# Three-stage attention: scores per head, raw probabilities turned, a column of ones beside the values

## The chip, the cores and the metric

One core of one Trainium2 chip runs the whole program. The metric is the device time of one execution in microseconds (us).

## What is computed

Two blocks run one after the other on 256 tokens of width 1024, in float32. The first has two layers. Layer 0 mixes the tokens by a sparse attention with three branches (compressed, selected, window; called NSA here), layer 1 by a block attention on shared keys (MoBA); each is followed by a mixture of 32 experts and a gated embedding (PLE). The second block has a feed-forward part, a mixer (half pooling, half dilated attention) and another feed-forward part, all modulated by a vector. At 256 tokens each of the three attentions reads all its causal keys, so the part that the change rewrites is, for every head,

```python
s = q @ k.T - slopes * dist
s = jnp.where(mask, s, -jnp.inf)
e = jnp.exp(s - m)
o = (e / jnp.maximum(jnp.sum(e, axis=axis, keepdims=True), 1e-30)) @ v
```

with 16 heads of 64 in NSA (two such branches and the compressed one, each times its gate, are added) and in MoBA, and 8 heads in the mixer, where the exponentials are also multiplied by a table of weights (several dilations fall on the same key).

## The kernel before

The weights stream in by DMA on SyncE's queue into nine buffers of 2048 columns (tag `raw`). Dense products (L305 to L307) split both factors into a high and a low part and take three passes of matmuls. Instructions are recorded in program order, and a scheduler then sets the order on each engine; K holds its hints. Matmuls that have nothing to do with attention stand among the attention's: compressed scores (L698, L716), the transposes of the normalised queries (L348), pieces of the modulation vector (L1448, L1461, called by `fill`), and products with the output weights as soon as an eighth of the input is there.

Attention works in units of two neighbouring heads (index `j`) and one branch. NSA has 8 pairs with two branches, 16 units; MoBA has 8 units, the mixer 4. Queries lie turned, the dimensions of both heads on 128 partitions. `keys` makes a tile with two copies of the keys, each with zeros in place of the other head's 64 dimensions (L545 on GpSimd, POOL), so that one matmul with 128x128 weights gives the scores of both heads: L566 for the first 128 queries and keys, L568 for the other queries and all 256 keys. Then, unit by unit:

- VectorE (DVE) adds slope times distance and takes the minimum in one instruction per block (L575, four blocks: 128 or 256 keys, two heads). ScalarE (ACT) takes the exponential and the sum of each row (L580); in the mixer DVE multiplies by the table and sums (L583).
- DVE turns the sums into factors w (L586, L587; L589 multiplies NSA's gate into them), and the probabilities are scaled by w in place: one block on ACT (L593), three on DVE (L595).
- The matrix engine (PE) turns them by six transposes (L599 to L601), and ACT copies them out of PSUM (L602, two copies).
- `attend` (L609, L611) multiplies with the values as weights, 64 columns for each head, so that the two heads fill the two halves of the output partitions and the result is already turned. In NSA the second branch and the compressed one (L782, tiles of 32 rows) add into the same PSUM tile. `parts` (L300 on ACT, L301 on DVE) splits it for the product with the output weights.

`pair` (L773) does this for NSA, loops in `moba` (L831) and `mixer` (L1580) for the others. After pair 1 the second half of the queries is normalised, turned and put through the compressed softmax (`q_norm`, `q_T`, `compressed_softmax`), which puts a chain of DVE work between the units. PSUM has two sets of four banks, `psa` (scores) and `psb`.

Of the kernel before, what the change touches and what calls it, by code (L numbers as in the profile page):

```python
# [43 lines left out]
    sw='svvv',  # L44
# [153 lines left out]
class Block:  # L198
# [343 lines left out]
    def keys(self):  # L542
        kb = self.raw.tile([P, 4, 2, T], F32, tag="raw", name="kb")
        for hf in range(2):
            self.nc.gpsimd.memset(kb[64 * hf:64 * hf + 64, :, 1 - hf], 0.0)  # L545
        return kb

    def put_k(self, idx, ps, gain):

        nc = self.nc  # L550
        for hf, eng in ((0, "s"), (1, "v")):
            sl = slice(64 * hf, 64 * hf + 64)
            dst = self.KB[idx // 4][sl, idx % 4:idx % 4 + 2, hf, :]
            if gain is None:
                self.copy(dst, ps[sl])
            elif eng == "s":
                nc.scalar.activation(dst, ps[sl], AF.Identity, scale=gain[sl])
            else:
                nc.vector.tensor_scalar(dst, ps[sl], gain[sl], None, op0=OP.mult)

    def softmax_T(self, j, kb, QT, slopes, dist, mult, gate):

        nc = self.nc
        with self.ahead_by("soft"):
# [5 lines left out]
            p = self.pp_p.tile([P, 6 * P], F32, tag="p", name="p")  # L570
            p0, p1 = p[:, 0:2 * P].rearrange("p (h k) -> p h k", h=2), p[:, 2 * P:].rearrange("p (h k) -> p h k", h=2)
            blocks = [(p0[:, 0], s0[:, 0], P, 2 * P), (p0[:, 1], s0[:, 1], P, 2 * P),
                      (p1[:, 0], s1[:, 0], 0, 2 * P), (p1[:, 1], s1[:, 1], 0, 2 * P)]
            for i, (p, s, a, b) in enumerate(blocks):
                nc.vector.tensor_tensor_reduce(out=p, in0=s, in1=dist[:, a:b], scale=-float(slopes[2 * j + i % 2]),  # L575
                                               scalar=3e38, op0=OP.add, op1=OP.min, accum_out=m[:, i:i + 1])
            den = self.stat([P, 4], "den")
# [142 lines left out]
    def nsa(self):  # L720
# [74 lines left out]
        for j in range(8):  # L795
            pair(j)
            if j == K["norm_a"]:
                self.q_norm(q[1])
# [869 lines left out]
```

## Time and profile before

| | us |
|---|---|
| median of 3 runs (lowest to highest) | 1142.69 (1141.37 to 1143.42) |
| the profiled execution | 1141.74 |
| its span, first to last instruction | 1139.9 |
| PE busy (of the span) | 1061.5 (93%) |
| weight loads (PEld) busy | 830.7 (73%) |
| DVE busy | 729.1 (64%) |
| ACT busy | 514.6 (45%) |
| POOL busy | 74.8 (7%) |
| mean granted clock of PE | 0.973 of full |

Matmuls overlap, and the end of each in the trace is modelled, so differences between starts tell what a stream of them costs. A float32 matmul takes two passes and leaves two records, a transpose one. A wait on PEld is one of a weight load, which comes ahead of its matmul.

### The profile page before, as it was taken

To read this page: it belongs to the slowest core of one execution; us is meant where nothing else is said; L and a number is where in the kernel's file an instruction comes from. 1 tells how busy PE (TensorE), PEld (TensorE's weight loads), DVE (VectorE), ACT (ScalarE), POOL (GpSimd) and SP (SyncE) were. 2 spreads that over 40 slices of the span, in tenths; PEclk is the share of its full clock that TensorE was granted. 3 is DMA by queue.
4 is the path that set the end of the run, shared out by engine and by line. 5 is a ranking of instruction groups with operands and counts; after the bars stand their busy time and mean duration, and the time that the engine had idled before them with its cause. 6 is when DMAs were issued, how large, how long until landed. Compare 5 with 4: busy or idle time off the path is not lost.

```text
span 1139.9 us, 18296 instructions
## 1 busy us (share of the span) xinstructions
PE 1061.5 (93%) x7037; PEld 830.7 (73%) x7037; DVE 729.1 (64%) x1717; ACT 514.6 (45%) x992; POOL 74.8 (7%) x61
## 2 busy tenths in 40 slices
PE   7997999998899899998987999999989979999995
PEld 5884557564467667665555999999879759999994
DVE  6787866542379957343377587878674776554555
ACT  5446774221267774321253443443544634444443
POOL 3000002100010002000003000000210030000001
PEclk9998999997999999999998999999989989999998
DMA  9755464899964635898886468786674344454401
GB/s 372 287 194 223 186 231 154 300 383 371 350 245 166 245 126 187 327 372 318 333 322 265 148 239 332 302 308 252 234 300 168 129 184 145 169 189 164 141 26 38
DMA packets 46507, 268.55 MB, mean 236 GB/s; under 512 B 5328, under 2 KB 7120, under 8 KB 20432
## 3 DMA queue, kind: packets, MB, share of 16 engines
q1 hardware_dynamic: 46416, 267.34, 62.4%
q8 instruction: 57, 0.93, 0.3%
q14 instruction: 34, 0.28, 0.1%
HBM read 266.27 MB, written 1.05 MB: 235 GB/s over the span
## 4 chain that ended last, share of the span: by engine, by line
PE 47%; DVE 5%; ACT 1%; issue 0%; ACTq 0%; DVEq 0%
PE b L306 8%; PE b L305 8%; PE b L307 8%; PE a L305 5%; PE a L307 5%; PE a L306 5%; PE a L1055 1%; DVE nq L320 1%; PE b L1461 1%; DVE h L1484 1%; PE a L1095 1%; PE a L1108 1%; DVE rstd L324 1%; DVE w L1483 1%; PE b L1034 0%
## 5 line engine op out<-in xcount | busy, mean ns | idle before, releaser
L293 DVE TENSOR_TENSOR lo<-raw,hi 128x1024 fp32r<-128x1024 f32 (+2 forms) x220 | 255.9, 1167 | 166.5 <-ACT hi L292 165.7
L292 ACT ACTIVATE hi<-raw 128x1024 fp32r<-128x1024 f32 (+2 forms) x234 | 234.3, 1008 | 266.2 <-PE b L306 142.5
L305 PE MATMUL b<-e,hi 128*128 128x256 f32 x768 | 219.8, 286 | 2.9 <-ACT e L427 2.9
L306 PE MATMUL b<-e,hi 128*128 128x256 f32 x768 | 219.5, 286 | 0.1
L307 PE MATMUL b<-e,lo 128*128 128x256 f32 x768 | 219.1, 285 | 0.0
L305 PE MATMUL a<-hi,e 128*128 128x512 f32 (+2 forms) x512 | 201.5, 394 | 2.4 <-ACT e L365 1.8
L307 PE MATMUL a<-hi,e 128*128 128x512 f32 (+2 forms) x512 | 198.4, 390 | 0.5 <-DVE e L366 0.5
L306 PE MATMUL a<-lo,e 128*128 128x512 f32 (+2 forms) x512 | 198.9, 388 | 0.0
L305 PEld LDWEIGHTS b<-e,hi 128*128 128x128 f32 x768 | 149.4, 195 | 3.9 <-ACT e L427 3.6
L306 PEld LDWEIGHTS b<-e,hi 128*128 128x128 f32 x768 | 149.4, 194 | 1.0 <-DVE e L428 0.7
L307 PEld LDWEIGHTS b<-e,lo 128*128 128x128 f32 x768 | 149.3, 194 | 0.0
L305 PEld LDWEIGHTS a<-hi,e 128*128 128x128 f32 x512 | 97.4, 190 | 23.2 <-ACT e L365 2.9
L307 PEld LDWEIGHTS a<-hi,e 128*128 128x128 f32 x512 | 96.7, 190 | 21.3 <-DVE e L366 2.1
L306 PEld LDWEIGHTS a<-lo,e 128*128 128x128 f32 x512 | 97.6, 191 | 19.0 <-DVE lo L293 0.9
L1055 PE MATMUL a<-raw,e 128*32 128x256 f32 x832 | 78.6, 399 | 5.5 <-PEq L1314 5.4
L1055 PEld LDWEIGHTS a<-raw,e 128*32 128x32 f32 x832 | 32.2, 113 | 23.9 <-issue 9.0
L1439 DVE SCALAR_TENSOR_TENSOR w<-raw,c,w 128x512 f32<-128x512 f32 x63 | 45.7, 747 | 0.6
L485 DVE TENSOR_TENSOR h<-h,a 128x512 f32<-128x512 f32 x48 | 31.9, 684 | 21.0 <-PE a L1108 14.4
L580 ACT ACTIVATE p<-p,m 128x128 f32<-128x128 f32 (+1 forms) x96 | 42.6, 447 | 5.5 <-DVE m L575 4.4
L293 POOL TENSOR_TENSOR lo<-raw,hi 128x1024 fp32r<-128x1024 f32 (+1 forms) x14 | 31.4, 2263 | 206.1 <-ACT hi L292 206.0
L1098 ACT ACTIVATE w<-a,sv 128x512 fp32r<-128x512 f32 x32 | 21.6, 687 | 50.0 <-PE a L1095 49.0
L1084 ACT ACTIVATE hb<-a,rr 128x128 f32<-128x128 f32 x16 | 6.0, 373 | 83.6 <-DVE rr L1024 77.2
(321 smaller groups left out, 1455.9 us busy)
## 6 DMA issues: line engine op xcount, KB each, us to landing
raw<-in_ffn SPq DMA_DIRECT2D x62, 1024.0 KB, 4.8
raw<-in_moe_gu SPq DMA_DIRECT2D x52, 1024.0 KB, 7.3
raw<-in_w_ada SPq DMA_DIRECT2D x36, 1024.0 KB, 6.7
wd<-in_moe_dn SPq DMA_DIRECT2D x64, 512.0 KB, 6.1
raw<-in_w_gate SPq DMA_DIRECT2D x8, 1024.0 KB, 10.8
raw<-in_w_m_in SPq DMA_DIRECT2D x8, 1024.0 KB, 7.3
raw<-in_w_a_in SPq DMA_DIRECT2D x7, 1024.0 KB, 11.0
e<-in_moe_gu SPq DMA_DIRECT2D x6, 1024.0 KB, 6.7
```

The source lines that it names most:

```text
L292: nc.scalar.activation(hi[:, sl], raw[:, at], AF.Copy)
L293: eng.tensor_tensor(lo[:, sl], raw[:, at], hi[:, sl], op=OP.subtract)
L305: mm(out, l[0], r[0], start=start, stop=False, **kw)
L306: mm(out, l[0], r[1], start=False, stop=False, **kw)
L307: mm(out, l[1], r[0], start=False, stop=stop, **kw)
L320: nc.vector.scalar_tensor_tensor(q, y, h, y, op0=OP.mult, op1=OP.mult)
L324: nc.vector.scalar_tensor_tensor(y, q, 1.5, y, op0=OP.add, op1=OP.mult)
L485: self.nc.vector.tensor_tensor(self.h[:, t, sl], self.h[:, t, sl], ps, op=OP.add)
L580: nc.scalar.activation(p, p, AF.Exp, bias=m[:, i:i + 1], scale=-1.0, accum_out=den[:, i:i + 1])
L1055: nc.tensor.matmul(pgs[pp][32 * x:32 * x + 32], xg[:, k, o:o + 32], wg[kk][:, x], start=(k == 0), stop=(k == KT - 1))
L1098: nc.scalar.activation(yh[:, sl], py, AF.Identity, scale=cw)
L1439: eng.scalar_tensor_tensor(rows, w, by, rows, op0=OP.mult, op1=OP.add)
```

## The change

`softmax_T` and `attend` give way to one function, `attention`, which runs a list of units through three stages: the scores of unit i, the transposes of unit i-1, the products of unit i-2, and then whatever stands beside it (`beside`: the fills and the second half of the queries).

- Scores are four matmuls over 64 rows each, for each head and each half of the queries, into one PSUM tile a head; the first half of the queries meets 128 keys only. The keys are stored once, without zeros, so `keys` loses its two POOL fills, and `put_k` writes all 128 partitions in one instruction (in NSA one buffer holds both branches).
- The exponentials keep no sums and are turned unscaled. `values` puts a column of ones behind each head's 64, so that the product (L607 to L609, turned probabilities as weights, 65 columns moving) brings the sum along with the output, queries on partitions. DVE takes the maximum with 1e-30, the reciprocal and the gate (L611, L612, L614) and scales the output out of PSUM (L616).
- In NSA POOL adds the two branches (L618), and the sum is turned by a matmul against the identity (L811) into the PSUM tile into which the compressed branch was multiplied (L808, as L782 before). In MoBA and the mixer two transposes (L639) turn it.
- Small tiles are shared to make room (`le`, `full`).

```diff
-    def softmax_T(self, j, kb, QT, slopes, dist, mult, gate):
...
-            s0 = self.psa([P, 2, P])
-            nc.tensor.matmul(s0, QT[:, j, 0:P], kb[:, :, 0:P], start=True, stop=True)
-            s1 = self.psa([P, 2, T])
-            nc.tensor.matmul(s1, QT[:, j, P:T], kb, start=True, stop=True)
...
+    def keys(self, n):
+        kb = self.raw.tile([P, n, 4, T], F32, tag="raw", name="kb")
+        self.KB = [kb[:, i] for i in range(n)]
...
+    def values(self, groups, tail):
+        n = 2 * groups * 65
+        t = self.e([P, 2064])
+        v = t[:, 0:n].rearrange("p (t g d) -> p t g d", t=2, d=65)
+        self.nc.gpsimd.memset(v[:, :, :, 64:65], 1.0)
+        return v, t[:, n:n + tail]
+
+    def attention(self, units, QT, slopes, dist, mult, finish, beside):
...
+        def scores(u):
+            j, kb, _, _, _ = units[u]
+            s = [self.psa([P, 3 * P]) for _ in range(2)]
+            for t in range(2):
+                for hh in range(2):
+                    sl = slice(64 * hh, 64 * hh + 64)
+                    mm(s[hh][:, t * P:t * P + (t + 1) * P], QT[sl, j, t * P:(t + 1) * P], kb[sl, 0:(t + 1) * P],
+                       start=True, stop=True)
...
+            for i, (o, x, a) in enumerate(blocks):
+                nc.scalar.activation(o, o, AF.Exp, bias=m[:, i:i + 1], scale=-1.0)
+                if mult is not None:
+                    nc.vector.tensor_tensor(o, o, mult[:, a:2 * P], op=OP.mult)
+            live[u] = p
+
+        def turn(u):
...
+                for k in range(3):
+                    nc.tensor.transpose(ps[:, k * P:(k + 1) * P], p[:, hh, k * P:(k + 1) * P], self.ident)
+                nc.scalar.activation(pT[:, hh], ps, AF.Copy)
...
+        def products(u):
+            j, _, v, gate, last = units[u]
+            pT = live.pop(u)
+            ps = self.psb([P, 2, 2, 65])
+            for hh in range(2):
+                mm(ps[:, 0, hh], pT[:, hh, 0:P], v(0, hh), start=hh == 0, stop=True, skip_group_check=True)
+                mm(ps[:, 1, hh], pT[:, hh, P:2 * P], v(0, hh), start=False, stop=False, skip_group_check=True)
+                mm(ps[:, 1, hh], pT[:, hh, 2 * P:], v(1, hh), start=False, stop=True, skip_group_check=True)
+            w = self.stat([P, 2, 2, 1], "w")
+            nc.vector.tensor_scalar(w, ps[:, :, :, 64:65], 1e-30, None, op0=OP.max)
+            nc.vector.reciprocal(w, w)
+            if gate is not None:
+                nc.vector.tensor_tensor(w[:, :, :, 0], w[:, :, :, 0], gate, op=OP.mult)
+            o = self.wk.tile([P, 2, 2, 64], F32, tag="xn", name="o", bufs=4)
+            nc.vector.tensor_tensor(o, ps[:, :, :, 0:64], w.to_broadcast([P, 2, 2, 64]), op=OP.mult)
+            if j in rows:
+                nc.gpsimd.tensor_tensor(o, o, rows.pop(j), op=OP.add)
+            if last:
+                finish(j, o.rearrange("p t h d -> p t (h d)"))
+            else:
+                rows[j] = o
+
+        n = len(units)
+        for i in range(n + 2):
+            if i < n:
+                scores(i)
+            if 1 <= i <= n:
+                turn(i - 1)
+            if i >= 2:
+                products(i - 2)
+            beside(i)
...
             for hh in range(2):
...
+                nc.tensor.matmul(oT[64 * hh:64 * hh + 64], self.VC[c:c + 32, g], PC[c:c + 32, g], start=True, stop=False,
+                                 skip_group_check=True)
+            for t in range(2):
+                nc.tensor.matmul(oT[:, t * P:(t + 1) * P], o[:, t], self.ident, start=False, stop=True,
+                                 skip_group_check=True)
             self.parts(aT[0][:, j], aT[1][:, j], oT)
```

Where the instructions stand. In these listings, names read output<-inputs: `a` and `b` are PSUM tiles, `kb` keys, `e` on a score matmul the queries and on a product the values, `p` and `pT` probabilities before and after turning; `consts` holds the identity and the distances.

The first listing is PE in the opening of NSA, behind the first scores; before:

```order
L568 MATMUL a<-kb,e 128x512
L566 MATMUL a<-kb,e 128x256
L568 MATMUL a<-kb,e 128x512
L1448 MATMUL a<-raw,c_701 32x512 x8
L566 MATMUL a<-kb,e 128x256
L716 MATMUL b<-consts,pc 128x128 x2
L568 MATMUL a<-kb,e 128x512
L716 MATMUL b<-consts,pc 128x128 x2
L566 MATMUL a<-kb,e 128x256
L599 MATMUL b<-consts,p 128x128
L600 MATMUL b<-consts,p 128x128
```

and now:

```order
L577 MATMUL a<-kb,e 128x128
L577 MATMUL a<-kb,e 128x256 x2
L577 MATMUL a<-kb,e 128x128 x2
L577 MATMUL a<-kb,e 128x256 x2
L1484 MATMUL a<-raw,c_693 32x512
L746 MATMUL b<-consts,pc 128x128 x2
L598 MATMUL b<-consts,p 128x128 x3
L746 MATMUL b<-consts,pc 128x128 x2
L598 MATMUL b<-consts,p 128x128 x3
L1484 MATMUL a<-raw,c_693 32x512 x7
L577 MATMUL a<-kb,e 128x128 x2
```

The scores of two units now stand in front, pieces of the modulation and the compressed products (L716, now L746) come later, and the first transposes stand between and behind the two compressed products; the third unit's scores follow them.

The second listing is PE in the steady part of NSA, with the numbers of the tiles; before:

```order
L601 MATMUL b_1264<-consts_88,p_1245 128x128
L599 MATMUL b_1269<-consts_88,p_1245 128x128
L600 MATMUL b_1269<-consts_88,p_1245 128x128
L601 MATMUL b_1269<-consts_88,p_1245 128x128
L1461 MATMUL b_1297<-consts_88,w4_1295 128x1 x4
L609 MATMUL b_1201<-pT_1263,e_240 64x256 x2
L611 MATMUL b_1201<-pT_1263,e_240 64x128 x2
L782 MATMUL b_1201<-e_240,vc_96 64x256 x2
```

and now:

```order
L808 MATMUL b_1464<-e_240,vc_96 64x256 x2
L577 MATMUL a_1471<-kb_457,e_689 128x128
L577 MATMUL a_1472<-kb_457,e_689 128x128
L577 MATMUL a_1471<-kb_457,e_689 128x256
L577 MATMUL a_1472<-kb_457,e_689 128x256
L811 MATMUL b_1464<-consts_88,o_1461 128x128 x2
L598 MATMUL b_1488<-consts_88,p_1430 128x128 x3
L598 MATMUL b_1493<-consts_88,p_1430 128x128 x3
L607 MATMUL b_1498<-e_240,pT_1439 128x65
L608 MATMUL b_1498<-e_240,pT_1439 128x65
L609 MATMUL b_1498<-e_240,pT_1439 128x65
```

Before, only a piece of the modulation (L1461) stands between the transposes of `p_1245` and the products with `pT_1263`, which is the same unit. Now the products behind the transposes of `p_1430` are with `pT_1439`, turned from the unit ahead of it (`p_1390`), and the second output step L811 stands behind one unit's scores.

The third listing is DVE in the same place; before:

```order
L586 TENSOR_SCALAR den_1352<-den_1352 128x4
L575 ISA p_1414,m_1413<-a_1411,consts_88 128x256
L575 ISA m_1413 128x1
L587 RECIPROCAL w_1357<-den_1352 128x4
L589 TENSOR_TENSOR w_1357<-w_1357,gates_242 128x4
L595 TENSOR_SCALAR p_1347<-p_1347,w_1357 128x128
L595 TENSOR_SCALAR p_1347<-p_1347,w_1357 128x256 x2
L586 TENSOR_SCALAR den_1419<-den_1419 128x4
L587 RECIPROCAL w_1424<-den_1419 128x4
L589 TENSOR_TENSOR w_1424<-w_1424,gates_242 128x4
L595 TENSOR_SCALAR p_1414<-p_1414,w_1424 128x128
L595 TENSOR_SCALAR p_1414<-p_1414,w_1424 128x256
```

and now:

```order
L584 ISA p_1430,m_1429<-a_1423,consts_88 128x256
L584 ISA m_1429 128x1
L584 ISA p_1430,m_1429<-a_1424,consts_88 128x128
L584 ISA m_1429 128x1
L584 ISA p_1430,m_1429<-a_1424,consts_88 128x256
L584 ISA m_1429 128x1
L611 TENSOR_SCALAR w_1457<-b_1450 128x4
L612 RECIPROCAL w_1457<-w_1457 128x4
L614 TENSOR_TENSOR w_1457<-w_1457,gates_243 128x4
L616 TENSOR_TENSOR o_1461<-b_1450,w_1457 128x256
L584 ISA p_1478,m_1477<-a_1471,consts_88 128x128
L584 ISA m_1477 128x1
```

L595 is gone. The small operations L611 to L614 and the scaled copy L616 now stand behind the minima of the unit whose scores PE made before these products, and ahead of the next unit's.

## Rows read from the trace of the kernel before

**Rows 1.** The page's first part: busy us, share of the span, instructions.

```profile
PE 1061.5 (93%) x7037; PEld 830.7 (73%) x7037; DVE 729.1 (64%) x1717; ACT 514.6 (45%) x992; POOL 74.8 (7%) x61
```

**Rows 2.** Busy by stretch: us, PE, PEld, DVE, ACT, POOL, PEclk, DMA share, GB/s.

```profile
84.90:170.50 85.60, 78.64 (x478) 45.20 (x478) 62.48 (x302) 61.48 (x202) 0.00 (x0) 0.96 0.56 213
384.00:423.00 39.00, 32.70 (x173) 21.00 (x173) 28.81 (x135) 31.00 (x104) 0.00 (x0) 1.00 0.55 205
883.60:907.60 24.00, 23.71 (x127) 17.16 (x126) 20.87 (x97) 16.95 (x40) 0.00 (x0) 1.00 0.28 106
```

**Rows 3.** Waits of the DMA queue, 150 to 320 us: us, times, longest us.

```profile
SPq L275 <- PE a L1055: 35.9, 13, 6.3
```

**Rows 4.** Waits of the weight loads in NSA: us, times, longest us.

```profile
PEld b L599 <- ACT p L593: 7.5, 5, 5.1
PEld b L609 <- ACT pT L602: 5.7, 12, 0.8
```

**Rows 5.** Waits of the weight loads in MoBA.

```profile
PEld b L609 <- ACT pT L602: 4.9, 14, 0.7
PEld b L599 <- ACT p L593: 4.5, 4, 2.3
```

**Rows 6.** Waits of the weight loads in the mixer.

```profile
PEld b L609 <- ACT pT L602: 2.0, 6, 0.5
```

**Rows 7.** Timeline, PE in the mixer: start us, us, instruction.

```profile
888.85 0.60 PE L566 MATMUL a<-kb,e 128*128 128x256 f32 x2
889.28 1.02 PE L568 MATMUL a<-kb,e 128*128 128x512 f32 x2
890.14 0.59 PE L1576 MATMUL b<-pool,w 128*128 128x256 f32 x2
...
892.95 0.27 PE L599 MATMUL b<-consts,p 128*128 128x128 f32 x1
...
893.49 0.27 PE L601 MATMUL b<-consts,p 128*128 128x128 f32 x1
894.06 0.81 PE L609 MATMUL b<-pT,e 128*64 128x256 f32 x3 [0.29 <-ACT pT L602]
```

**Rows 8.** Timeline, PE in NSA's opening: idle before in brackets.

```profile
104.75 0.69 PE L599 MATMUL b<-consts,p 128*128 128x128 f32 x2 [4.62 <-ACT p L593]
```

**Rows 9.** Busy by stretch around that wait, columns as rows 2.

```profile
99.70:104.80 5.10, 0.48 (x5) 0.05 (x1) 5.00 (x29) 5.00 (x16) 0.00 (x0) 0.73 0.39 165
104.80:108.50 3.70, 3.39 (x14) 1.98 (x14) 2.93 (x8) 1.27 (x3) 0.00 (x0) 0.50 0.27 35
```

**Rows 10.** Timeline, PE in NSA's steady part.

```profile
129.87 0.95 PE L1461 MATMUL b<-consts,w 128*128 128x1 f32 x8
130.75 0.65 PE L609 MATMUL b<-pT,e 128*64 128x256 f32 x4
131.24 0.39 PE L611 MATMUL b<-pT,e 128*64 128x128 f32 x4
131.55 0.65 PE L782 MATMUL b<-e,vc 32*64 32x256 f32 x4
```

**Rows 11.** Groups by shape in NSA: busy us, mean ns, idle before, releaser.

```profile
L580 ACT ACTIVATION_READ_ACCUMULATOR p<-p,m 128x1 f32 x64 | 12.2, 191 | 0.0
...
L595 DVE TENSOR_SCALAR p<-p,w 128x256 f32<-128x256 f32 x32 | 9.9, 347 | 0.0
...
L593 ACT ACTIVATE p<-p,w 128x128 f32<-128x128 f32 x16 | 6.3, 396 | 1.8 <-DVE w L589 1.8
...
L595 DVE TENSOR_SCALAR p<-p,w 128x128 f32<-128x128 f32 x16 | 4.5, 282 | 0.3
...
L587 DVE RECIPROCAL w<-den 128x4 f32<-128x4 f32 x16 | 2.8, 174 | 0.2
...
L701 DVE TENSOR_TENSOR pc<-a,consts 128x256 f32<-128x256 f32 x4 | 1.6, 420 | 0.3 <-PE a L698 0.2
```

**Rows 12.** Groups by shape on POOL, whole span.

```profile
L1005 POOL TENSOR_TENSOR G<-G,G 128x256 fp32r<-128x256 f32 x16 | 11.7, 731 | 158.9 <-DVE G L1003 141.4 <-DVE slg L1189 9.1 <-DVE rr L1025 6.1
```

More of the change, by code (lines that the diff above doesn't have):

```diff
@@ L605, in attend @@
-    def attend(self, oT, pT, v, start, stop):
-        mm = self.nc.tensor.matmul
-        for hh in range(2):
-            mm(oT[64 * hh:64 * hh + 64, :], v(0, hh), pT[:, hh, 0:T], start=start, stop=False)
-        for hh in range(2):
-            mm(oT[64 * hh:64 * hh + 64, P:T], v(1, hh), pT[:, hh, T:], start=False, stop=stop)
+            live[u] = pT
+        def products(u):
[17 more added lines that the diff above has]
+                finish(j, o.rearrange("p t h d -> p t (h d)"))
+            else:
+                rows[j] = o
@@ new lines, in attention, with out_T, put @@
+        n = len(units)
[7 more added lines that the diff above has]
+            beside(i)
+    def out_T(self, aT, j0):
+        def put(j, o):
+            oT = self.psb([P, T])
+            for t in range(2):
+                self.nc.tensor.transpose(oT[:, t * P:(t + 1) * P], o[:, t], self.ident)
+            self.parts(aT[0][:, j0 + j], aT[1][:, j0 + j], oT)
+        return put
@@ L763, in nsa @@
         next(compress)
-        self.KB = [self.keys() for _ in range(2)]
+        self.keys(2)
         self.k_T(0, ks, self.s("a_k_norm1"))
@@ L794, in nsa @@
         aT = (self.e([P, KT, T], F32R), self.e([P, KT, T], F32R))
[L795 to L798, printed above, removed]
-            if j == K["early_a"]:
-                self.q_T(QT, 1, q[1], qg)
-                self.compressed_softmax(1, QT, gates, PC)
-            self.fill("nsa", j)
-            if j == K["proj"]:
-                self.project_load(0)
+        units = [(j, self.KB[br][:, j // 2], lambda t, hh, br=br, g=j // 2: V[:, br, t, g],
+                  gates[:, :, 2 * j:2 * j + 2, 1 + br], br == 1) for j in range(8) for br in range(2)]
+        self.attention(units, QT, self.slopes, self.c("dist"), None, out, beside)
         self.moe(0, aT, "w_a_out")
@@ L830, in moba, with beside @@
         aT = (self.e([P, KT, T], F32R), self.e([P, KT, T], F32R))
-        for j in range(8):
-            g = j // 2
-            oT = self.psb([P, T])
-            pT = self.softmax_T(j, self.KB[0][:, g], QT, self.slopes, self.c("dist"), None, None)
-            self.attend(oT, pT, lambda t, hh: V[:, t, 64 * g:64 * g + 64], True, True)
-            self.parts(aT[0][:, j], aT[1][:, j], oT)
-            if j == K["norm_b"]:
+        def beside(i):
+            if i > 7:
+                return
+            if i == K["norm_b"]:
                 self.q_norm(q[1])
-            if j == K["early_b"]:
+            if i == K["early_b"]:
                 self.q_T(QT, 1, q[1], qg)
-            self.fill("moba", j)
-            if j == K["proj"]:
+            self.fill("moba", i)
+            if i == K["proj"]:
                 self.project_load(1)
+        units = [(j, self.KB[0][:, j // 2], lambda t, hh, g=j // 2: V[:, t, g], None, True) for j in range(8)]
+        self.attention(units, QT, self.slopes, self.c("dist"), None, self.out_T(aT, 0), beside)
         self.moe(1, aT, "w_b_out")
@@ L1197, in moe @@
         gate_up(0, 0, 3)
-        w, full, n_full, first = self.route_rest(i, Mb, L, gm, top)
+        w, full, n_full, first = self.route_rest(i, Mb, L, gm, top, tab["bias"][:, 0:32])
         if K["sv"]:
```

121 lines of the change are left out of this document (46 added, 75 removed).

## The prediction

> **What bounds the kernel now.** I read the page first: the matrix engine (PE) is busy for 1061.5 of 1139.9 us [rows 1], so PE's work and PE's waits make the time. The change touches three stretches. In the table by stretches PE is busy for 78.64 of 85.60 us in the first attention (NSA), 32.70 of 39.00 in the second (MoBA) and 23.71 of 24.00 in the mixer's [rows 2]: 7.0, 6.3 and 0.3 us are open there. Behind the first attention the loads of the experts' weights wait for buffers that PE's matmuls release, 35.9 us in 13 waits [rows 3]; a later PE means later loads, so I let a shift of an attention's end pass on one to one.
>
> Next, the waits. In NSA the weight loads wait 7.5 us for the scaled probabilities (L593, 5 times, once 5.1) and 5.7 us for the turned ones (L602, 12 times) [rows 4]; in MoBA it is 4.5 (4 times) and 4.9 (14) [rows 5], in the mixer 2.0 for the turned ones (6) [rows 6]. A transpose's modelled record lasts 0.27 us while one starts every 0.11 (892.95 to 893.49 is five steps [rows 7]), so each wait hides some 0.16 us in the busy share: 17 x 0.16 = 2.7 more in NSA, 18 x 0.16 = 2.9 in MoBA, 1.0 in the mixer. **Open time: 9.7, 9.2 and 1.3 us.** The longest wait has a second price. PE was idle for 4.62 us before 104.75 [rows 8], and from 104.8 to 108.5 the granted clock was 0.50, which is 1.2 of 2.4 GHz, with 3.39 us of busy PE [rows 9]. At full clock that work takes about half: 1.8 us more, so NSA has 11.5 to win.
>
> **PE's work in one unit** (two heads, one branch; 28 units: 16 in NSA, 8 in MoBA, 4 in the mixer), as differences of starts.
> Removed: L566, 0.43, and L568, 0.86 (888.85, 889.28, 890.14 [rows 7]); the four attend matmuls, 0.80 (130.75 to 131.55 [rows 10]). With six transposes of 0.11, 0.65, and 0.1 for changing between whole-array and half-array work (an estimate: 893.49 to 894.06 [rows 7] holds such a change, one transpose and a wait of 0.29), a unit is 2.84.
> Added, the scores: four matmuls over 64 rows each, of 128, 128, 256 and 256 columns. No row of before shows two row halves that fill all output partitions. One bound is that they run one behind the other, as long as L566 and L568: 1.29. The other comes from the attend. Four L609 records of 256 columns would take 4 x 0.215 = 0.86 in turn and took 0.49 (130.75 to 131.24 [rows 10]), so two column halves run side by side; row halves side by side would need 0.64. L782 works in tiles of 32 rows, and its four records of 256 columns end 0.65 after the first start [rows 10], which speaks for side by side too, though its tiles differ in columns as well. I take side by side, with 0.11 for a first weight load and 0.2 for two changes of mode: 0.95.
> Added, the products: six matmuls of two passes, each of which loads 128 columns of turned probabilities and moves 65. Eight L1461 records with 128x128 weights and one moving column take 0.88 us (129.87 to 130.75 [rows 10]): the load sets 0.11, whatever moves. 12 x 0.11 = 1.34, against 0.80 for the attend. The Trainium skill, "TensorEngine Tiling (Array Packing)", section "When to Use Tiling", advises the reverse of this step: with a moving side of 64 or less, swap the operands and tile the columns. The attend of before is that form, and the trace agrees that it is the cheaper one.
> Added, turning the output: in NSA two matmuls of two passes against the identity for a pair of branches, elsewhere two transposes, 0.22 a unit either way. With the transposes' 0.65 a unit is now 3.16, **0.32 more: NSA +5.1, MoBA +2.6, mixer +1.3.** L782 stays as it is (L808).
>
> **The other engines.** VectorE (DVE) loses L595, 2 x 0.347 + 0.282 = 0.98, and gains one scaled copy out of PSUM, priced as L701, 0.42 [rows 11]; maximum, reciprocal and gate stay with other inputs. ScalarE (ACT) loses four accumulator reads of 0.191 and L593, 0.396: 1.16 a unit [rows 11]. The mixer's masked multiply only loses its sums. The key tile's zero fills on POOL and the split key copies lie beside weight matmuls: nothing, and if that cover were gone half a microsecond. POOL gains eight additions, 0.731 each by L1005 [rows 12]. SP's list keeps its length and its place: nothing. Neither DVE nor ACT is full, so all this shortens chains and pays only where PE waits.
>
> **What becomes of the waits.** In the steady part the transposes and the products that follow each other on PE now belong to different units (the second listing), so the copy between them has a unit of cover: I let the 32 waits for L602 go. The waits for L593 go only as far as they are its own. In the long one DVE was busy for 5.00 of 5.10 us [rows 9], and of its queue there only the scaling leaves. Late next is the second output step, L811, which wants the scaled copy and POOL's addition. Between a pair's last product and L811 PE has L808 (0.58 by L782) and the next scores (0.95), 1.53 us; the chain is maximum, reciprocal and gate (0.17 each, by L587 [rows 11]), 0.42 and 0.73, so 1.66 us and what lies before it in DVE's queue. Stepping by hand through the new order with these durations, I let NSA keep 6.0 us in its opening (the first listing is its head; I got 3.5 to 8.1, by how DVE's small operations fall between the second half's normalisation and compressed softmax) and 1.5 at L811 (five waits of 0.3), 7.5 in all. MoBA keeps 1.2 at its head, where the first scores wait for the queries, and 1.5 for filling and draining three stages, 2.7. The mixer keeps 1.0.
>
> **Sum.** NSA +5.1 - 11.5 + 7.5 = +1.1; MoBA +2.6 - 9.2 + 2.7 = -3.9; mixer +1.3 - 1.3 + 1.0 = +1.0; together -1.8. The profiled execution took 1141.74 us, 0.95 under the median of the three runs, 1142.69. **1141.74 - 1.8 = 1139.9 us**, 2.8 under that median; 0.2% (2.3 us) is about what a measurement can tell from no change.
>
> **Rivals.**
> *The row halves run in turn.* Scores cost 0.64 more a unit, 28 x 0.64 = 17.9: 1157.8. For it: no row shows this shape. Against it: L609 and L782, and the two halves write two tiles of PSUM. The Trainium skill, "TensorE: Matmul & The Clock Gate", "Part 3: Packing small matmuls", says that matmuls on different row groups overlap; no run here shows that for halves yet.
> *The output's return becomes the wait (slower).* Place: L811, eight times in NSA. Price: if maximum to gate lie behind other work in DVE's queue for as long as PE's cover lasts, PE stands for the whole copy and addition, 0.42 + 0.73 = 1.15 a pair, 9.2 us instead of 1.5: 1147.6. It decides once the chain with its queue is over about 2.7 us (1.53 + 1.15). For it: in the third listing these small operations stand right behind the four minima (L584) of the unit before. Against it: those minima read scores that PE finished 2.0 us before the products' end (transposes 0.65, products 1.34), so they should be done, and the next unit's stand behind.
> *The pipeline takes nearly every wait.* If two thirds of the 11.2 us kept go too: 1132.4. For it: the shorter chains, 1.16 on ACT and 0.56 on DVE a unit, and no stand long enough to lose the clock. Against it: the opening's DVE queue.
> *Work and waits cancel.* NSA keeps 8.1 in its opening and MoBA 4.0 in all, 3.4 more than I let them: 1143.3.
>
> **Numbers.** The band of my forecast, 1137 to 1144, has 0.50, with the cancelling case in its upper part; nearly every wait gone (1128 to 1137) 0.18, the output's return (1144 to 1152) 0.20, row halves in turn (1152 to 1160) 0.12. Faster by over 0.2% is under 1140.4: 0.18 and half of 0.50, 0.43. Within 0.2%, to 1145.0: the other half and 0.01 of the next, 0.26. Slower: 0.31. The range 1131 to 1155 takes in the price of every rival but the row halves' and leaves out some 0.13.
>
> **What would show it.** Records of L577 on the two row halves that start within some 0.02 us, not 0.1 or 0.2 apart; records of L607 to L609 every 0.11 us; no weight load of L607 that waits for the copy (L599) in the steady part; L811 waiting under 0.4 us each; PE's clock full after 105 us; NSA's end about 1 us later and MoBA's stretch 4 shorter. It is wrong if L577 costs over 1.2 us a unit, if L811 waits over 1 us a pair, or if the experts' stages don't follow the shift.

## The result, and the profile after

The changed kernel took **1172.84 us**, median of four runs, of which three lie from 1166.70 to 1173.20 and one, of 5814 us, is left out of the ratio; the kernel before took 1142.03 beside it. The ratio is 1.0250, 95% interval 1.0209 to 1.0292. That is 30 us slower, where 1139.9 was forecast, and outside the range (1131 to 1155).

The page's first part, and its row of granted clocks in 40 slices, for the changed kernel:

```profile
PE 1085.3 (93%) x7317; PEld 864.8 (74%) x7317; DVE 719.0 (61%) x1641; ACT 495.6 (42%) x864; POOL 73.4 (6%) x64
...
PEclk9899799999999879999999899999989998999998
```

Against [rows 1] PE is busy 24 us longer, DVE 10 and ACT 19 us shorter. The shares say little; the stretches say more. The three attentions of the changed kernel, columns as in [rows 2]:

```profile
97.10:193.80 96.70, 89.94 (x634) 64.89 (x635) 57.11 (x268) 50.30 (x122) 5.81 (x8) 0.93 0.48 178
410.60:454.20 43.60, 39.55 (x250) 32.38 (x251) 24.19 (x116) 24.08 (x63) 0.00 (x0) 0.80 0.57 217
905.20:939.00 33.80, 33.26 (x197) 27.27 (x197) 24.51 (x76) 19.89 (x39) 0.00 (x0) 1.00 0.45 156
```

NSA starts at 97.1 where it started at 84.4, and MoBA's stretch has a clock of 0.80 where [rows 2] had 1.00. So I cut both traces at the same marks (starts of PE instructions): the first compressed score; the first transposes of the expert stage's norm (L880 before, L917 now); the last L1108 (L1144); MoBA's first score; the second L880; the first L420 (L419) of the feed-forward part; the L1475 (L1511) behind the mixer; the end. Three kernels of the experiments stand beside them:

| us from mark to mark | before | changed | one-column fill | head by head | full-array scores |
|---|---|---|---|---|---|
| up to NSA | 84.4 | 97.1 | 85.8 | 85.5 | 85.1 |
| NSA | 99.0 | 111.3 | 110.1 | 105.1 | 104.8 |
| experts | 137.2 | 127.2 | 127.2 | 127.3 | 127.8 |
| up to MoBA | 65.0 | 75.0 | 65.3 | 65.3 | 65.6 |
| MoBA | 50.0 | 56.1 | 55.5 | 46.9 | 47.8 |
| second experts | 175.6 | 175.8 | 173.9 | 175.8 | 175.6 |
| feed-forward, mixer | 296.3 | 296.1 | 294.8 | 293.3 | 295.3 |
| last feed-forward | 232.4 | 231.6 | 232.2 | 233.5 | 231.6 |
| span | 1139.9 | 1170.2 | 1144.8 | 1132.7 | 1133.6 |

The 30.3 us of span are +12.7 and +10.0 *ahead* of the two first attentions, where the prediction had costed nothing, +12.3 and +6.1 in them, and -10.0 in the experts' stage, which the prediction had let pass every shift on (experiment 10 shows what these 10 us are). The mixer's stretch looks longer only because other work now lies in it: its row of the table is level.

**Ahead of the attentions.** PE's timeline in the changed kernel; in brackets, the idle time before an instruction and what ended it:

```profile
42.17 1.47 PE L672 MATMUL b<-raw,e 128*64 128x256 f32 x12
46.38 0.44 PE L682 MATMUL b<-consts,x 128*128 128x128 f32 x2 [2.74 <-DVE x L679]
...
55.29 2.12 PE L347 MATMUL b<-consts,w 128*128 128x128 f32 x8 [2.29 <-DVE w L535]
58.15 0.87 PE L304 MATMUL a<-hi,e 128*128 128x304 f32 x2 [0.73 <-ACT hi L291]
...
380.49 2.12 PE L347 MATMUL b<-consts,w 128*128 128x128 f32 x8 [4.77 <-DVE w L535]
```

And the kernel before at the first of these places:

```profile
41.65 1.68 PE L642 MATMUL b<-raw,e 128*64 128x256 f32 x14
43.26 0.41 PE L305 MATMUL a<-hi,e 128*128 128x304 f32 x1
```

Before, the 304-column dense product (L305 to L307) follows at once and fills the time in which DVE prepares the keys. Now the turning of the keys (L347, eight transposes) and the small matmuls before it stand ahead of that product on PE, and PE waits for DVE. The stretch that follows, by engines, in the changed kernel:

```profile
47.00:60.50 13.50, 9.43 (x37) 7.86 (x38) 9.93 (x44) 4.75 (x12) 0.00 (x0) 0.53 0.36 148
```

and before:

```profile
47.00:60.50 13.50, 13.38 (x107) 13.01 (x106) 11.13 (x46) 8.57 (x19) 0.00 (x0) 1.00 0.99 407
```

PE does 37 matmuls instead of 107. Its clock fell to half behind the 2.74 us stand, and the loads, whose queue waits 15.1 us for a split of weights on DVE (L292), run at 148 GB/s instead of 407. Ahead of MoBA it is the same with the 4.77 us at 380.49. The program order of these parts had not been touched, but the order on PE, DVE and ACT does differ there. DVE's, before (L293 splits the weights of that dense product; four pieces of 0.785 us):

```
L264 TENSOR_SCALAR e<-a,rstd 128x256 x2
L293 TENSOR_TENSOR lo<-raw,hi 128x608 x4
L646 TENSOR_SCALAR x_398<-x_398 128x256
```

and now, some 30 rows further down the list:

```
L535 TENSOR_TENSOR w_480<-w_242,knr 128x4x64 x4
L263 TENSOR_SCALAR kb<-b,small 128x512
L292 TENSOR_TENSOR lo<-raw,hi 128x608 x4
```

The split stands behind the first copy into the key tile, and so the dense product behind the whole chain of the key norm. For the prediction I had read the order in the attentions only. The edit that reaches this place is in `keys` and `put_k`: the fills are gone, and the key copies are one instruction.

**In the attentions.** PE's timeline in the changed kernel's steady part of NSA:

```profile
174.69 0.93 PE L577 MATMUL a<-kb,e 64*128 64x128 f32 x8
175.55 0.87 PE L598 MATMUL b<-consts,p 128*128 128x128 f32 x6
176.26 0.33 PE L607 MATMUL b<-e,pT 128*128 128x65 f32 x2
176.43 0.39 PE L608 MATMUL b<-e,pT 128*128 128x65 f32 x2
176.66 0.39 PE L609 MATMUL b<-e,pT 128*128 128x65 f32 x2
...
177.64 0.65 PE L808 MATMUL b<-e,vc 32*64 32x256 f32 x4
178.22 0.93 PE L577 MATMUL a<-kb,e 64*128 64x128 f32 x8
179.74 0.71 PE L811 MATMUL b<-consts,o 128*128 128x128 f32 x4 [0.59 <-POOL o L618]
180.29 0.82 PE L598 MATMUL b<-consts,p 128*128 128x128 f32 x6
```

A unit's scores take 0.86 us (174.69 to 175.55), its transposes 0.71, its products 1.38, two records every 0.22 or 0.23; the single records of the two row halves start 7 ns apart. All that is as forecast. Why the stretches still grew is what the experiments had to tell.

### The profile page after: what moved, and what is told of

It reads as the page before. It is cut to its first block, busy times and chain, and to the rows that moved or that the text cites. A ratio compares the mean times of both kernels' runs of the same rounds, so it can differ in the third digit from the quotient of the medians.

```text
span 1170.2 us, 18645 instructions
## 1 busy us (share of the span) xinstructions
PE 1085.3 (93%) x7317; PEld 864.8 (74%) x7317; DVE 719.0 (61%) x1641; ACT 495.6 (42%) x864; POOL 73.4 (6%) x64
## 4 chain that ended last, share of the span: by engine, by line
PE 45%; DVE 5%; ACT 1%; issue 0%; ACTq 0%; DVEq 0%
PE b L305 8%; PE b L304 8%; PE b L306 8%; PE a L304 5%; PE a L306 5%; PE a L305 5%; PE a L1091 1%; DVE nq L319 1%; PE b L1497 1%; DVE h L1520 1%; PE a L1131 1%; PE a L1144 1%; DVE rstd L323 1%; DVE w L1519 0%; PE b L1070 0%
## 5 line engine op out<-in xcount | busy, mean ns | idle before, releaser
L292 DVE TENSOR_TENSOR lo<-raw,hi 128x1024 fp32r<-128x1024 f32 (+2 forms) x220 | 255.9, 1168 | 163.1 <-ACT hi L291 162.3
L305 PE MATMUL b<-e,hi 128*128 128x256 f32 x768 | 217.9, 284 | 0.1
L305 PE MATMUL a<-lo,e 128*128 128x512 f32 (+2 forms) x512 | 201.4, 393 | 0.0
L304 PEld LDWEIGHTS b<-e,hi 128*128 128x128 f32 x768 | 147.0, 191 | 3.9 <-ACT e L426 3.6
L305 PEld LDWEIGHTS b<-e,hi 128*128 128x128 f32 x768 | 146.0, 190 | 1.1 <-DVE e L427 0.7
L306 PEld LDWEIGHTS b<-e,lo 128*128 128x128 f32 x768 | 146.2, 190 | 0.0
L305 PEld LDWEIGHTS a<-lo,e 128*128 128x128 f32 x512 | 98.2, 192 | 22.2 <-DVE lo L292 2.3
L1091 PE MATMUL a<-raw,e 128*32 128x256 f32 x832 | 73.7, 383 | 1.3 <-DVEq L1328 0.9
L292 POOL TENSOR_TENSOR lo<-raw,hi 128x1024 fp32r<-128x1024 f32 (+1 forms) x14 | 31.5, 2264 | 402.7 <-ACT hi L291 402.7
L587 ACT ACTIVATE p<-p,m 128x128 f32<-128x128 f32 (+1 forms) x112 | 45.2, 447 | 25.6 <-DVE m L584 25.4
L1475 DVE SCALAR_TENSOR_TENSOR w<-raw,c,w 128x512 f32<-128x512 f32 x63 | 45.6, 746 | 0.6
L1131 PE MATMUL a<-wd,hT 128*32 128x512 f32 x256 | 42.4, 600 | 0.0
## 6 DMA issues: line engine op xcount, KB each, us to landing
raw<-in_w_gate SPq DMA_DIRECT2D x8, 1024.0 KB, 11.2
```

What stands on the lines that cost most here:

```text
L292: eng.tensor_tensor(lo[:, sl], raw[:, at], hi[:, sl], op=OP.subtract)
L304: mm(out, l[0], r[0], start=start, stop=False, **kw)
L305: mm(out, l[0], r[1], start=False, stop=False, **kw)
L306: mm(out, l[1], r[0], start=False, stop=stop, **kw)
L587: nc.scalar.activation(o, o, AF.Exp, bias=m[:, i:i + 1], scale=-1.0)
L1091: nc.tensor.matmul(pgs[pp][32 * x:32 * x + 32], xg[:, k, o:o + 32], wg[kk][:, x], start=(k == 0), stop=(k == KT - 1))
```

## The experiments

In their order; each ratio is to the kernel before, timed beside it. The expectations were written before the runs.

**1. The fill put back.** All of the changed kernel, with one fill of the whole key tile that nothing needs.

```diff
         kb = self.raw.tile([P, n, 4, T], F32, tag="raw", name="kb")
+        self.nc.gpsimd.memset(kb, 0.0)
```

> Edit: the changed kernel, and POOL fills the key tile with zeros once before it is written. Theory A (order): without the fills the scheduler put the turning of the keys, and what waits for it, ahead of the weight splits and dense matmuls in front of each attention, and PE stands there; with a fill these stand as before. A expects the first compressed score (L728's successor) back from 97 to about 85 us, the stretch from MoBA's first key transpose to its first score back from 30 to about 16 us, and 1146 to 1158 us in all. Theory B (the attention itself is what costs): the stretches ahead come back but the attentions take the time, over 1163 us. Theory C (the loads, by one raw buffer less for keys): nothing moves, 1170 us or more, first compressed score still at 97.

1148.55 us, ratio 1.0045 (1.0028 to 1.0061). NSA starts at 85.8 and MoBA's first score comes 65.3 us behind the experts' last matmul, as before. So some 24 of the 30 us came from leaving out an instruction that looked free.

**2. The fill in NSA alone.**

```diff
+        if n == 2:
+            self.nc.gpsimd.memset(kb, 0.0)
```

> Edit: the changed kernel with the fill in NSA only. A expects NSA's start at about 85 us as with all fills, MoBA's stretch still about 30 us, and a time between the changed kernel and fill_back: the experts' stage had given back 15 of NSA's 24 us, so the NSA fill alone is worth 5 to 12 us, the other two 10 to 18. B expects no more than 4 us from it. C expects nothing.

1157.81 us, ratio 1.0145 (1.0109 to 1.0181). NSA starts at 86.2; ahead of MoBA the key transposes start at 368.3 and the first score follows only at 398.7, 30.4 us later, against 16.0 in the kernel before (369.6 to 385.6). Each place answers to its own fill. By the ratios NSA's is worth 12 us and the other two 11. (The 15 us in the expectation are what the experts' stage had left of NSA's shift; it had given back 10.)

**3. The key turning moved in the program.** No fill, but the calls of `k_T` stand behind the dense product that they had overtaken.

```diff
-        self.k_T(0, ks, self.s("a_k_norm1"))
         kw = self.w4([P, 2, 256])
         off = self.dense(x, "w_a_in", [304, 256], put_win, off)
+        self.k_T(0, ks, self.s("a_k_norm1"))
         self.k_T(1, kw, self.s("a_k_norm2"))
...
-        self.k_T(0, k, self.s("k_norm_shared"))
...
             if c == 0:
+                self.k_T(0, k, self.s("k_norm_shared"))
                 self.q_norm(q[c])
```

> Edit: the changed kernel without fills; the program turns NSA's selected keys behind the window's dense products and MoBA's keys behind the first half of the queries, so that the order comes from the program. A expects NSA's start within 3 us of fill_back's, MoBA's stretch near 16 to 20 us, and a time within 6 us of fill_back (the mixer is left as it is). If the fills matter in themselves (POOL's work, the buffer's release) it stays above 1165 us.

1169.91 us, ratio 1.0223 (1.0202 to 1.0245): a miss. NSA still starts at 94.7; PE stands 3.59 us up to 64.54 and 4.67 up to 392.12, again at the key transposes. The split of the weights is back in its old place, but the key transposes still come ahead of work that could cover them: moving the call only moved the stand.

**4. A fill of one column.** Is it the fill's time on POOL, or that there is one at all?

```diff
+        self.nc.gpsimd.memset(kb[:, :, :, 0:1], 0.0)
```

> Edit: as fill_back, but POOL writes one column of each key row instead of the whole tile (2048 columns become 8). If the order is all that the fill brings (theory A), the listing of every engine outside the fill is that of fill_back and the time is the same within 0.3%, 1145 to 1152 us. If POOL's work or the time at which the buffer is cleared matters, it falls back toward 1172.

1146.61 us, ratio 1.0045 (1.0028 to 1.0063), the same as the whole fill, and PE, DVE and ACT run the same instructions in the same order from start to end in both. It is the fill's being there that matters, not how long it takes. Why a first writer on POOL changes where the scheduler puts the key turning was read from the order only (with this fill the split of the weights stands where it stood before); what in the scheduler does it stays open.

What is left, 5 us slower than before, lies in the attentions (third column of the table): +11.1 in NSA and +5.5 in MoBA, with -10.0 in the experts' stage. PE's timeline of this kernel, rows with a long wait:

```profile
92.64 1.05 PE L1485 MATMUL a<-raw,c 128*32 128x512 f32 x2 [2.74 <-DVE m L585]
...
116.73 2.84 PE L1485 MATMUL a<-raw,c 128*32 128x512 f32 x10 [2.38 <-DVE m L585]
...
388.40 1.58 PE L578 MATMUL a<-kb,e 64*128 64x128 f32 x16 [1.08 <-DVE e L525]
391.23 0.69 PE L599 MATMUL b<-consts,p 128*128 128x128 f32 x2 [1.25 <-ACT p L588]
```

The modulation's matmuls (L1485) want a PSUM bank that a minimum (L585) of DVE has still to read. The changed kernel has the same two waits, 2.73 and 1.39 us, at 103.89 and 128.86.

**5. Row-half scores on the kernel before.** Before's softmax and attend, with the changed kernel's keys and scores and the one-column fill.

```diff
-            s0 = self.psa([P, 2, P])
-            nc.tensor.matmul(s0, QT[:, j, 0:P], kb[:, :, 0:P], start=True, stop=True)
-            s1 = self.psa([P, 2, T])
-            nc.tensor.matmul(s1, QT[:, j, P:T], kb, start=True, stop=True)
+            s = [self.psa([P, 3 * P]) for _ in range(2)]
+            for t in range(2):
+                for hh in range(2):
+                    sl = slice(64 * hh, 64 * hh + 64)
+                    nc.tensor.matmul(s[hh][:, t * P:t * P + (t + 1) * P], QT[sl, j, t * P:(t + 1) * P], kb[sl, 0:(t + 1) * P],
+                                     start=True, stop=True)
```

> Edit: the kernel before with the new scores alone: keys without zeros, four matmuls on row halves, the one-column fill; scaling, turning and the attend of two column halves stay as before. Theory D (the products are the dear step, the scores a gain): PE's work falls by 0.43 us a unit (1.29 to 0.86, as the changed kernel's trace shows), 12 us over 28 units, of which 4 to 10 show; 1132 to 1139 us. Theory E (PE's work in the attentions is covered by waits for VectorE, so that the scores' gain is lost): 1141 to 1145 us.

1143.93 us, ratio 1.0021 (1.0008 to 1.0034). Counted from start to start over the 28 units, with time at half clock taken at half, the scores cost PE 31 us where before they cost 39.5, and the kernel is no faster. Its experts' stage is even 9.7 us shorter than that of the kernel before (experiment 10), so its attentions are longer: in the profiled execution (1148.28 us) NSA takes 111.4 us (99.0 before) and MoBA 54.3 (50.0). Two rows of its timeline in NSA's opening:

```profile
91.69 1.06 PE L1441 MATMUL a<-raw,c 128*32 128x512 f32 x2 [2.74 <-DVE m L569]
...
108.51 0.69 PE L594 MATMUL b<-consts,p 128*128 128x128 f32 x2 [4.46 <-ACT p L587]
```

The second is the wait of [rows 8]; the first is new and came with the scores.

**6. The pair's output turned one unit later.** The one-column fill, and `finish` behind the next unit's transposes.

```diff
             if last:
-                finish(j, o.rearrange("p t h d -> p t (h d)"))
+                late.append(lambda: finish(j, o.rearrange("p t h d -> p t (h d)")))
...
+            while late:
+                late.pop()()
             if i >= 2:
```

> Edit: tiny, and the output of a pair is turned one unit later (behind the next unit's transposes), so that PE doesn't stand for the scaled copy and the addition on POOL. Theory F (the output's return is a new wait): the waits of weight loads for the addition, 4.9 us in NSA, go, and those for the scaled copy in MoBA too; 3 to 8 us faster than tiny, NSA's attention from 98 to about 93 us. Theory G (the rest is the dearer products and the low clock in the openings): within 2 us of tiny.

1145.68 us, ratio 1.0035 (1.0022 to 1.0048), against 1146.61 without it. The waits of MoBA's output transposes, 2.0 us in all, are gone. The times differ by 1 us, which the intervals don't tell from nothing: the return of the output is not where the time is.

**7. The minima head by head, on the kernel of experiment 5.** A row-half score tile holds both query halves of one head. In the order of blocks 0, 1, 2, 3 the first tile is free only after the third of the four minima; in the order 0, 2, 1, 3 it is free after two, as the tile of the first queries was in the kernel before.

```diff
-            for i, (p, s, a, b) in enumerate(blocks):
+            for i in (0, 2, 1, 3):
+                p, s, a, b = blocks[i]
```

> Edit: halves_old, with VectorE's four minima of a unit taken head by head instead of by halves of the queries, so that the first score bank is free after two of them. In halves_old PE stood 3.1 and 2.0 us in NSA's opening at matmuls of the modulation that wait for a score bank, where the kernel before doesn't stand. Theory J (a bank of row-half scores is freed later, since it holds both halves of the queries of one head): these waits fall by 1 us or more each and low-clock time in NSA falls with them; 1137 to 1142 us. Theory K (VectorE's chain of the compressed softmax is what they wait for): the waits stay within 0.5 us and the time within 2 us of halves_old.

1140.17 us, ratio 0.9971 (0.9960 to 0.9983), half a per cent under experiment 5, for an edit that removes no instruction. The order of the minima is part of the price of row halves. That it is so because a tile is held longer is argued, not shown: the waits at the modulation's matmuls, 2.74 and 1.39 us in experiment 5, are 2.38 and 1.42 here and did not fall by 1 us each as that theory wanted. What fell between the two profiled executions is NSA's time at half clock, from 27 to 10 us.

**8. The same on the changed kernel** (experiment 6's, with the same edit in `attention`).

```diff
-            for i, (o, x, a) in enumerate(blocks):
+            for i in (0, 2, 1, 3):
+                o, x, a = blocks[i]
```

> Edit: late_out with the minima head by head. J: 2 to 5 us faster than late_out, 1141 to 1144 us. K: within 2 us of it.

1141.58 us, ratio 0.9995 (0.9970 to 1.0020), 4 us under experiment 6 as expected, but from 1134.45 to 1150.34 over eight runs of one program, almost in the order of the mean granted clock: 0.979 at the fastest, 0.970 in the middle, 0.963 at the slowest. The profiled run is that of 1134.45 us. Its MoBA, beside that of experiment 6 (profiled at 1148.43 us), suggests what that hangs on. Timeline and stretch of experiment 6:

```profile
391.84 1.58 PE L578 MATMUL a<-kb,e 64*128 64x128 f32 x16 [1.08 <-DVE e L525]
394.69 0.69 PE L599 MATMUL b<-consts,p 128*128 128x128 f32 x2 [1.26 <-ACT p L588]
```

```profile
391.00:432.00 41.00, 38.86 (x246) 31.99 (x247) 24.36 (x117) 24.47 (x63) 0.00 (x0) 0.79 0.53 187
```

and of this kernel:

```profile
383.19 1.58 PE L578 MATMUL a<-kb,e 64*128 64x128 f32 x16 [1.09 <-DVE e L525]
386.03 0.33 PE L600 MATMUL b<-consts,p 128*128 128x128 f32 x1 [1.25 <-ACT p L589]
```

```profile
384.00:418.00 34.00, 32.08 (x246) 26.41 (x244) 23.09 (x115) 23.02 (x61) 0.00 (x0) 1.00 0.62 216
```

The same two stands, 1.1 and 1.25 us; behind them the clock fell in the one and held in the other, and the stretch took 41 or 34 us.

**9. Full-array scores with the new softmax.** Experiment 6 with before's keys, fills, key copies and score matmuls; transposes, products, ones and output stay as changed.

```diff
-            s = [self.psa([P, 3 * P]) for _ in range(2)]
-            for t in range(2):
-                for hh in range(2):
...
+            s0 = self.psa([P, 2, P])
+            mm(s0, QT[:, j, 0:P], kb[:, :, 0:P], start=True, stop=True)
+            s1 = self.psa([P, 2, T])
+            mm(s1, QT[:, j, P:T], kb, start=True, stop=True)
...
-            blocks = [(p[:, hh, t * P:t * P + (t + 1) * P], s[hh][:, t * P:t * P + (t + 1) * P], (1 - t) * P)
+            blocks = [(p[:, hh, t * P:t * P + (t + 1) * P], (s0, s1)[t][:, hh], (1 - t) * P)
```

> Edit: late_out with the scores of before (zero-filled keys, two full-array matmuls a unit), so the new products alone. Theory D (PE's work decides): 0.43 us a unit more than late_out, 12 us, of which 6 or more show: 1151 us or more. Theory H (what the attentions lose is the clock that falls when the scores are short and PE stands): low-clock time in MoBA falls from 17 us to under 7, and the time stays within 3 us of late_out, 1143 to 1149 us.

1135.41 us, ratio 0.9938 (0.9917 to 0.9958): faster than both theories allowed. By the count of experiment 5 the scores are some 9 us more work for PE, and the kernel is 10 us faster than experiment 6, with no time at half clock in MoBA. So the row halves, with the keys, copies and fills that belong to them, are not a gain here but a loss. The Trainium skill, "TensorEngine Tiling (Array Packing)", section "When to Use Tiling", advises two row tiles for a contraction of 64; the matmuls do run side by side here, and the kernel is slower with them and what belongs to them (1145.68 against 1135.41).

**10. The same without the late output**: the changed kernel with nothing but before's keys and scores.

```diff
-                late.append(lambda: finish(j, o.rearrange("p t h d -> p t (h d)")))
+                finish(j, o.rearrange("p t h d -> p t (h d)"))
```

> Edit: wide_new without the delay of the output, so the changed kernel with the scores (and keys and fills) of before and all else as it is. Theory H (the row-half scores and the order are the whole loss): 1135 to 1140 us, no low clock in MoBA. If the delayed output is what made wide_new fast: 1143 us or more, with PE standing at the output's turn in MoBA.

**1134.22 us**, ratio 0.9926 (0.9909 to 0.9943), from 1133.55 to 1135.42: faster than both kernels, and the last column of the table. Its page and its three attentions:

```profile
PE 1068.2 (94%) x7205; PEld 852.6 (75%) x7205; DVE 721.7 (64%) x1645; ACT 497.2 (44%) x868; POOL 81.2 (7%) x72
```

```profile
85.10:175.20 90.10, 86.77 (x570) 62.97 (x571) 57.40 (x268) 50.77 (x122) 6.13 (x8) 0.98 0.55 203
383.30:418.60 35.30, 33.62 (x218) 27.26 (x219) 23.90 (x116) 23.76 (x63) 0.00 (x0) 1.00 0.57 209
877.20:902.00 24.80, 24.80 (x149) 20.52 (x148) 18.43 (x72) 15.69 (x37) 0.00 (x0) 1.00 0.28 105
```

**11. Row halves in the mixer alone**, where PE never stands (experiment 9, minima head by head there).

```diff
-        self.keys(1)
+        self.keys(1, False)
...
+            if self.wide:
+                s0 = self.psa([P, 2, P])
...
+                order = (0, 1, 2, 3)
+            else:
+                s = [self.psa([P, 3 * P]) for _ in range(2)]
...
+                order = (0, 2, 1, 3)
```

> Edit: wide_new, with row-half scores and keys without zeros in the mixer alone, whose matrix work had kept its clock with either scores (23.7 us against 26.5 from the first score to the last output). H: the mixer's part falls by 2 to 3 us without low clock, 1131 to 1136 us in all. If row halves drop the clock anywhere: low-clock time after 877 us and no gain.

1135.92 us, ratio 0.9935 (0.9915 to 0.9956): no different from experiment 9. From its first score (878.2) to the mark behind it (901.4) the mixer takes 23.2 us, beside 26.0 in experiment 9 and 24.1 in 10, so a gain of a microsecond or two may be there; the runs do not show it.

**Where experiment 10 gains.** Not in its attentions: NSA is 5.8 us longer than before, MoBA and the mixer's row 2.2 and 1.0 shorter. It gains behind NSA, where the experts' stage is 9.4 us shorter, though all that was edited in it is where two small tiles lie (and experiment 5, without that edit, has 127.4 too). PE's timeline and two stretches of the kernel before, there:

```profile
259.75 1.52 PE L1108 MATMUL a<-w,GT 128*128 128x512 f32 x6
266.40 1.03 PE L1055 MATMUL a<-raw,e 128*32 128x256 f32 x2 [5.13 <-PEq L1314]
```

```profile
260.50:266.50 6.00, 0.87 (x5) 0.44 (x4) 1.28 (x2) 0.00 (x0) 0.00 (x0) 0.95 1.01 412
266.50:280.50 14.00, 14.00 (x73) 5.38 (x73) 2.42 (x9) 0.37 (x1) 1.45 (x2) 0.54 0.91 360
```

and the same place in experiment 10:

```profile
266.17 1.52 PE L1149 MATMUL a<-w,GT 128*128 128x512 f32 x6
268.52 0.62 PE L1096 MATMUL a<-raw,e 128*32 128x256 f32 x2 [0.84 <-DVEq L1333]
```

Before, PE stood for 5.13 us and then had a clock of 0.54 for 14 us; in experiment 10 it stands 0.84 and keeps its clock. What ended the long stand is PEq, PE's own sequencer (PEldq in the rows below), at L1314, the `If` around the loop over experts that are too full. Its branch there, in ns (shortest, median and longest of the two layers), in the kernel before and in experiment 10:

```profile
L1314 PEldq COMPARE_BRANCH x2: 334/2477/4620, 261.5 to 527.6; - x2
L1355 PEldq COMPARE_BRANCH x2: 218/276/334, 267.9 to 523.0; - x2
```

So PE did not wait for weights: the branch alone lasted from 261.46 to 266.08, and if the loads are used in the order in which they were issued, those of this matmul had landed at 240.01. Nor is it enough that the DMA engines are full (share 1.01 here): in experiment 10 they are as full around the same branch (1.02 from 262 to 268.5), and it takes 0.22 us. In the changed kernel and all eleven experiments this branch takes 0.21 to 0.44 us, and the stage lasts 127.2 to 129.5 us wherever NSA ends, from 189.4 to 208.4. The 10 us are a loss of the kernel before alone, and of all its runs, as far as times tell: 57 of them lie between 1138.95 and 1144.80 us, none near the 1132 that it would take without. Why its branch took so long is open; one 16 KB packet of the instruction queue moved meanwhile, at 263.70, but no run tests whether PE waited for it. Every ratio above has these 10 us in it (in experiment 11 it is 8), 0.9%: without them experiment 10 would be no faster than the kernel before, and the changed kernel some 40 us slower.

## Why the prediction was wrong, point by point

- **"The key tile's zero fills on POOL and the split key copies lie beside weight matmuls: nothing, and if that cover were gone half a microsecond."** This step failed, and it is the bulk of the miss: experiments 1 and 4 give back some 24 us. I had priced the instructions and not their place. The order ahead of both attentions changed with them, and the views that I rested on began where the attentions begin.
- **"NSA +5.1, MoBA +2.6, mixer +1.3" for PE's work.** About right in NSA, too much in the others. Counting each PE record up to the next one's start in the NSA stretch of experiment 4, scores, transposes, products and output take 56.9 us where before took 50.9: +5.9. The row halves run side by side; the scores are 0.86 in the steady part and 1.11 on the mean, for 0.95; the products 1.37 for 1.34; the output 0.28 for 0.22. In experiment 8, at full clock in both places, the same count gives +0.8 in MoBA and some +0.7 in the mixer: the products of before, taken as 0.80, cost 1.14 and 1.06 there. So the first rival (row halves in turn) falls, though its time was the nearest.
- **The waits: NSA 11.5 open and 7.5 kept, MoBA 9.2 and 2.7.** By the same count PE's idle time, with half of its time at 1.2 GHz added, was 10.4 us before in the NSA row of the table and 5.2 in MoBA's (the share that I took as hidden in the records is not in this count). In experiment 10 it is 5.0 and 1.7, so with full-array scores the pipeline does what I let it do. In experiment 4 it is 11.2 and 12.1 (8.5 of it clock): with the changed kernel's own scores nothing is won. What failed is "Stepping by hand ... I let NSA keep 6.0 us in its opening", and in MoBA a clock of 1.00 taken for granted. Shorter scores let PE reach its waits sooner, and both score tiles are held up to the last two minima; I counted the first as a gain and did not see the second. This reading is argued from the order; experiment 7 shows only that the order of the minima counts.
- **"I let a shift of an attention's end pass on one to one."** Right as a rule, among the twelve kernels without the long branch: their stage has the same length wherever NSA ends. It missed by the 10.0 us that the kernel before alone loses there, which nothing in the prediction had seen. That they fell the changed kernel's way is luck. The 35.9 us of [rows 3] are waits of loads for PE; they say nothing of this stand, in which PE waits for its own sequencer.
- **"The output's return becomes the wait."** A rival that fell. The waits for POOL's addition at L811, of the weight load and of PE itself, in the changed kernel's NSA (us, times, longest):

```profile
PEld b L811 <- POOL o L618: 4.9, 7, 1.0
...
PE b L811 <- POOL o L618: 1.4, 3, 0.6
```

  PE itself stands 1.4 us, the 0.59 shown above among them, near the 1.5 in all that I kept; experiment 6 takes most such waits out and gains 1 us at the most. From the last product to L811 the chain takes some 2.05 us, not 1.66, each small operation handing over for 0.04 to 0.2 us more than its own time.
- **The signs to look for.** The halves' starts, 0.11 us from product to product, and no waits for the copy held. "PE's clock full after 105 us", "NSA's end about 1 us later" and "MoBA's stretch 4 shorter" did not; MoBA came out shorter only in experiments 8 to 11, by 2.2 to 3.4 us. None of the signs looked ahead of 84 us, where the first 12.7 were lost.

No rival had the place.

**Open.** Why short scores leave the clock so often at 1.2 GHz: stands of equal length (experiments 6 and 8) came out both ways, and I have no run that separates the stand from the work around it. In the kernel before MoBA has a stand of 2.02 us, up to 399.56, and its clock is 1.00 throughout. Open as well: what in the scheduler ties the key turning to the fill, and what held PE's branch in the kernel before.

## What to carry to other kernels

An edit that only removes a cheap instruction can still move the order of everything that shares its tile: compare the whole order on each engine, not the region that the diff is about, and give the first difference outside it a price. Work that is taken from the busiest engine pays only if what it waits for next is not late; here some 8 us of shorter scores were worth less than nothing, since the engine then stood, and lost its clock. And when a stage that nobody edited gets shorter, ask what ended the stand that is gone before you credit the change: here it was a branch of the engine's own sequencer, and without its 10 us the best kernel of the experiments would have no lead.

## What the hardware showed that I had not expected

- The time of one and the same program goes with its granted clock: that of experiment 8 ran from 1134.45 us (mean clock 0.979) to 1150.34 (0.963). The Trainium skill, "TensorE: Matmul & The Clock Gate", "A second HAM failure mode: psum-queue depth-cycling", tells of frequent short idles between groups of matmuls, at the PSUM banks, that let the clock swing. Experiment 6's MoBA agrees in part: stands of 1.08 and 1.26 us, none longer, and a clock of 0.79; but they are only two, and they wait for DVE and ACT. Experiment 8's, with the same stands and 1.00, shows that it need not happen.
- Matmuls on two halves of the rows, with outputs in two PSUM tiles, start 7 ns apart: four of them (128, 128, 256 and 256 columns, float32) take 0.86 us, where the 768 columns of the two full-array matmuls took 1.29 [rows 7]. That this made no kernel here faster was the surprise.
- One branch of PE's sequencer took 4.62 us in the kernel before and 0.21 to 0.44 us in the twelve other kernels; in its own second layer it took 0.33. With the clock of 0.54 in the 14 us behind it, it cost some 10 us.
